# Tying wide products between transposes in TensorE's order: a two-layer decoder trunk

## The chip, the cores and the metric

The kernel runs as one program on one core of a Trainium2 chip; the other cores are idle. The metric is device time in microseconds (us) of one execution, lower is better. Three runs of the kernel before took 705.88, 707.46 and 708.49 us; the median is 707.46.

A core has five instruction queues that matter here: PE (TensorE, the matrix engine), DVE (VectorE), ACT (ScalarE), POOL (GpSimd) and SP (which issues the DMAs). Each queue is served in the order in which the program was written out; an instruction whose operand is not ready holds everything behind it on its engine.

## The reference

512 tokens of width 1024 run through two layers, in F32. Cut to what matters:

```python
def even_layer(x, mem_n, ...):
    h = rms_norm(x, norm_g)
    a_u, a_v, a_g, b_q, b_k, b_v, b_g, m_q, m_g = split_cols(h @ w_in, EVEN_SPLITS)
    y_a = chunked_sgu(gelu(a_u), gelu(a_v), ...) * silu(a_g)       # 4 groups, chunks of 128
    o_b = rms_norm(diff_attention(q, k, v, lam), b_subln) * ...    # 8 heads, two maps each
    y_b = o_b * silu(b_g)
    y_m = memory_attention(m_q, mem_n, ...) * silu(m_g)            # 4 heads over 256 memory tokens
    return x + concatenate([y_a, y_b, y_m]) @ w_out

def odd_layer(x, mem_n, ...):
    h = rms_norm(x, norm_g)
    c_a, c_b, c_g, d_q, d_kv, d_bg, d_g, m_q, m_g = split_cols(h @ w_in, ODD_SPLITS)
    y_c = conformer_conv(c_a, c_b, ...) * silu(c_g)                # causal depthwise conv, 31 taps
    y_d = nsa(d_q, kv, gates, ...) * silu(d_g)                     # compressed, selected and window attention
    y_m = memory_attention(m_q, mem_n, ...) * silu(m_g)
    return x + concatenate([y_c, y_d, y_m]) @ w_out
```

## The kernel before

**Two kinds of products.** F32 accuracy is made from a faster type. A matrix is split into a high part, rounded to F32R, and a low part, the rest (`split`, L375 to L377: the high part on ACT, L376, the low part on DVE, L377; weights in `load_unit`, the high part on ACT, L386, the low part on POOL, L389). One product then is three matmuls into the same bank of PSUM: high x high (L402), high x low (L403), low x high (L404). Their moving operand is 512 columns wide as a rule, in some units 256, 280 or 384. These are the wide products. Beside them stand matmuls whose stationary operand, the one that is loaded into the array before the other streams through, is plain F32 with 128 columns: the transposes (`tr`, L399, 128 moving columns), the products of attention weights and values of layer 0 (L965, 64 columns), the spatial gate (L856) and a few of the convolution's norm. A plain F32 product that is no transpose runs in two passes, so that 3649 matmuls of the program are 3819 in the trace.

**Stages.** Layer 0 opens with projections; then its differential attention (`b_attn`) runs head by head with the remaining projections as filler, memory attention (`m_attn`) with the first part of the output projection, and the rest of that projection. Layer 1 follows the same pattern: projections and convolution, memory attention, then sparse attention (`d_attn`) with gates and output projection as filler. An attention step is a chain over the engines: scores on PE (L927), the masked maximum on DVE (L929, which also empties the bank), exp on ACT (L958 and L1190), a scaling on DVE, transposes on PE (L399), `split`, value products on PE (L965 or L1213). A gate is a projection, a tanh on ACT (L478) and one DVE operation (L479), after which its bank is free.

**What sets the order.** `emit` writes the work as generators that `merge` interleaves by weights (FILL0 and the like). A scheduler then lays out each engine's queue from its own estimate of when an instruction is ready and how long it takes. Data dependences become semaphore waits. SBUF and PSUM are handed out by the kernel's own arenas, so a bank or page that is used again is a dependence too. No line of the kernel before names PE's order as such.

Of the kernel before, what the change touches and what calls it, by code (L numbers as in the profile page):

```python
# [23 lines left out]
F32 = mybir.dt.float32  # L24
F32R = mybir.dt.float32r
# [6 lines left out]
P = 128  # L32
S = 512
DM = 1024
# [248 lines left out]
        self.close()  # L283


def emit(ctx, tc, nc, D, out):
    sbp = ctx.enter_context(tc.tile_pool(name="sb", bufs=1))
    psp = ctx.enter_context(tc.tile_pool(name="ps", bufs=1, space=bass.MemoryType.PSUM))
    words = {k: sum(a * b for c in v.values() for a, b in c) for k, v in PAGES.items()}
# [12 lines left out]
    def banks(d, s, t, o):  # L302
        arenas["p"].deal(512, d=d, s=s, t=t, o=o)

    V, A, G, mm = nc.vector, nc.scalar, nc.gpsimd, nc.tensor.matmul
    dma = nc.sync.dma_start
    act = A.activation

    def f32(t):
        return t.bitcast(F32)  # L310

    def bc(ap, shape):
        return ap.broadcast_to(list(shape))

    def tok(i):
        return slice(i * P, (i + 1) * P)
# [4 lines left out]
    def load_x():  # L321
        for i in range(NT):
            x_t[i] = x_sc([P, DM])
            dma(x_t[i], D["x"][tok(i), :])

    def load_gain(j, sc):
        t = sc([P, DM])
        dma(t, bc(D["norms"][j:j + 1, :], [P, DM]))
        return t
# [3 lines left out]
    for a in range(2):  # L333
        dma(x_t[0][:, a * 512:(a + 1) * 512], D["x"][tok(0), a * 512:(a + 1) * 512])
    gain0 = load_gain(1, start_sc)
    coff = [0]

    def C(shape):
        n = int(np.prod(shape[1:]))
        v = cst_t[:shape[0], coff[0]:coff[0] + n]  # L340
        coff[0] += n
        assert coff[0] <= CONST
        if len(shape) == 3:
            v = v.rearrange("p (a b) -> p a b", a=shape[1])
# [34 lines left out]
    def load_unit(sc, dram, w=DM, eng=None):  # L379
        u = sc([P, 2, DM], F32R, "w")  # L380
        h, l = u[:, 0, :w], u[:, 1, :w]
        with SC() as rs:
            raw = rs([P, w], F32, "raw")
            dma(raw, dram)
            if eng is None:
                act(h, raw, AF.Copy)  # L386
                for a in range(0, w, 512):
                    c = slice(a, min(a + 512, w))
                    G.tensor_tensor(l[:, c], raw[:, c], f32(h[:, c]), SUB)  # L389
            else:  # L390
                split(raw, h, l, eng)
        return h, l

    def load(sc, name):
        i, n = UIDX[name]
        return [load_unit(sc, D["wall"][i + j]) for j in range(n)]

    def tr(o, i, k=P):
        nc.tensor.transpose(o, i, ident[:k, :k])  # L399

    def mm3(o, lh, ll, rh, rl, first, last):
        mm(o, lh, rh, start=first, stop=False)  # L402
# [3 lines left out]
    def h_tile(xt, gain, hs, tk, parts=1):  # L406
        with SC() as sc:
            xs = sc([P, DM])
            ss = sc([P, 2])
            cols = [slice(a * DM // parts, (a + 1) * DM // parts) for a in range(parts)]  # L410
            for a, c in enumerate(cols):
                act(xs[:, c], xt[:, c], AF.Square, accum_out=ss[:, a:a + 1])
            if parts == 2:
                G.tensor_tensor(ss[:, 0:1], ss[:, 0:1], ss[:, 1:2], ADD)
            r = rstd(sc, ss[:, 0:1], 1.0 / DM, 1)
            for c in cols:
                V.scalar_tensor_tensor(xs[:, c], xt[:, c], r, gain[:, c], MUL, MUL)  # L417
            for b in range(2):
                with SC() as pc:
                    p = pc.ps("t", [P, 4, P])  # L420
                    for k in range(4):
                        tr(p[:, k, :], xs[:, (4 * b + k) * P:(4 * b + k + 1) * P])
                    split(p, hs[0][b][:, :, tk], hs[1][b][:, :, tk])
# [90 lines left out]
    def to_keys(sc, t, r, _, h, l):  # L514

        d = sc([P, 4, 2, 64])
        V.tensor_tensor(d, bc(t.unsqueeze(2), [P, 4, 2, 64]),
                        bc(r.unsqueeze(2).unsqueeze(3), [P, 4, 2, 64]), MUL)
        p = sc.ps("t", [P, 4, P])
        for k in range(4):  # L520
            tr(p[:, k, :], d[:, k, :, :].rearrange("p a d -> p (a d)"))
        split(p, h, l)

    def to_queries(sc, q3, r, t, dst):

        nh = t.shape[1]
        V.tensor_tensor(t, q3, bc(r.unsqueeze(2), [P, nh, 64]), MUL)
        p = sc.ps("t", [P, nh // 2, P])
        for k in range(nh // 2):
            tr(p[:, k, :], t[:, 2 * k:2 * k + 2, :].rearrange("p a d -> p (a d)"))  # L530
        for n, q in enumerate(dst):
            q = q.rearrange("p (k a) t -> p a k t", a=2)
            for a in range(2):
                src = p[64 * a:64 * a + 64, 2 * n:2 * n + 2, :]
                act(q[0:64, a], src, AF.Copy)
                V.tensor_tensor(q[64:128, a], src, f32(q[0:64, a]), SUB)
# [815 lines left out]
                     out_part(1, srcs, rev, done)), 1.0)))  # L1352

PAGES = {"f": {"f": [(1024, 10), (512, 18), (16, 40)], "raw": [(1024, 3)]},
         "r": {"x": [(2048, 7)], "w": [(2048, 5)]},
# [20 lines left out]
ARRAYS = ["x", "mem", "wall", "wqb", "vec", "bs", "col", "w1", "w2", "wsT", "norms", "tab"]  # L1378


def build(shapes):
    nc = bacc.Bacc("TRN2", target_bir_lowering=False, num_devices=1)
    D = {n: nc.dram_tensor(f"in_{n}_dram", shapes[n], F32, kind="ExternalInput").ap() for n in ARRAYS}
    out = nc.dram_tensor("out_0_dram", (S, DM), F32, kind="ExternalOutput").ap()
    with tile.TileContext(nc, schedule_with_timeline_sim=True) as tc, ExitStack() as ctx:
        emit(ctx, tc, nc, D, out)
    return nc


# [5 lines left out]
```

## Time and profile before

| | |
|---|---|
| median of three runs | 707.46 us |
| the profiled execution | 707.62 us, its span 705.9 us |
| PE busy | 668.9 us (95%), 3819 matmuls |
| PE weight loads busy | 566.9 us (80%) |
| DVE, POOL, ACT busy | 496.9 (70%), 392.4 (56%), 377.1 us (53%) |
| chain that ended last | PE 70%, DVE 13%, POOL 5%, ACT 5%, issue 3%, DMA 3% |
| mean granted TensorE clock | 0.988 of full speed |

The span runs from the first instruction to the last. A matmul's recorded duration covers its whole way through the array, and matmuls overlap; what one costs PE is read from the distance between starts.

### The profile page before, as it was taken

The numbers are of one execution on the slowest core, as the hardware profiler recorded it, in microseconds if no ns is written. First come the engines' busy times: TensorE is split into PE (matmuls) and PEld (weight loads), VectorE is DVE, ScalarE is ACT, GpSimd is POOL, SyncE is SP. The second block draws the span as 40 slices with busy tenths as digits, with TensorE's granted clock in tenths as the row PEclk, the third lists the DMA queues.
The fourth block names the chain that finished last, engine by engine and source line by source line (L and its number), as shares of the span: only waits on it lengthen the run. The fifth ranks groups of instructions, "written<-read, shape, count | busy, mean of one in ns | idle before, by whom it ended". The sixth has DMA issues, their size and how long they took to land.

```text
span 705.9 us, 11050 instructions
## 1 busy us (share of the span) xinstructions
PE 668.9 (95%) x3819; PEld 566.9 (80%) x3819; DVE 496.9 (70%) x1204; ACT 377.1 (53%) x846; POOL 392.4 (56%) x414
## 2 busy tenths in 40 slices
PE   4999989999999979989989999899999999999997
PEld 3789989878888867878878888777777888788875
DVE  4605668666666875773465978998867776998773
ACT  5345345656455763752453568642346666676541
POOL 3367877474427773245754779965664523421650
PEclk9999999999999997999999999999999999999999
DMA  8532134463323252122322411104021101110121
GB/s 313 175 119 91 60 90 140 131 184 131 103 61 121 84 185 90 61 91 93 122 90 91 149 62 58 61 1 149 33 88 59 61 31 60 54 68 1 61 76 74
DMA packets 22376, 66.56 MB, mean 94 GB/s; under 512 B 3504, under 2 KB 3760, under 8 KB 22320
## 3 DMA queue, kind: packets, MB, share of 16 engines
q1 hardware_dynamic: 22320, 65.86, 28.5%
q8 instruction: 30, 0.49, 0.3%
q14 instruction: 26, 0.21, 0.1%
HBM read 57.46 MB, written 2.10 MB: 84 GB/s over the span
## 4 chain that ended last, share of the span: by engine, by line
PE 70%; DVE 13%; POOL 5%; ACT 5%; issue 3%; DMA 3%; SPq 0%; ACTq 0%; POOLq 0%; DVEq 0%
PE banks L403 18%; PE banks L404 17%; PE banks L402 17%; PE banks L399 6%; DVE arena_r L377 3%; PE banks L927 3%; DMA arena_f<-in_wall_dram 2%; POOL arena_r L389 2%; POOL arena_f L372 2%; PE banks L1213 2%; PE banks L965 2%; ACT arena_r L386 1%; DVE arena_f L929 1%; PE banks L1089 1%; PE banks L1183 1%
## 5 line engine op out<-in xcount | busy, mean ns | idle before, releaser
L389 POOL TENSOR_TENSOR arena_r<-arena_f,arena_r 128x512 fp32r<-128x512 f32 (+1 forms) x174 | 228.8, 1340 | 176.1 <-ACT arena_r L386 172.5
L402 PE MATMUL banks<-arena_r 128*128 128x512 f32 (+2 forms) x784 | 290.5, 375 | 5.4 <-ACT arena_r L386 2.2
L403 PE MATMUL banks<-arena_r 128*128 128x512 f32 (+2 forms) x784 | 290.9, 372 | 1.9 <-POOL arena_r L389 1.3
L404 PE MATMUL banks<-arena_r 128*128 128x512 f32 (+2 forms) x784 | 289.4, 371 | 1.5 <-DVE arena_r L377 1.5
L402 PEld LDWEIGHTS banks<-arena_r 128*128 128x128 f32 x784 | 149.3, 191 | 31.1 <-ACT arena_r L386 3.5
L403 PEld LDWEIGHTS banks<-arena_r 128*128 128x128 f32 x784 | 149.7, 191 | 25.4 <-POOL arena_r L389 2.8
L404 PEld LDWEIGHTS banks<-arena_r 128*128 128x128 f32 x784 | 149.4, 191 | 24.2 <-DVE arena_r L377 2.2
L386 ACT ACTIVATE arena_r<-arena_f 128x1024 fp32r<-128x1024 f32 (+2 forms) x87 | 91.1, 1049 | 75.6 <-PE banks L403 21.3
L399 PE MATMUL banks<-const,arena_f 128*128 128x128 f32 x507 | 84.1, 283 | 16.3 <-DVE arena_f L417 9.4
L377 DVE TENSOR_TENSOR arena_r<-banks,arena_r 128x512 fp32r<-128x512 f32 (+1 forms) x112 | 67.1, 608 | 27.4 <-ACT arena_r L376 26.9
L399 PEld LDWEIGHTS banks<-const,arena_f 128*128 128x128 f32 x507 | 63.0, 146 | 28.9 <-DVE arena_f L417 9.8
L376 ACT ACTIVATE arena_r<-banks 128x512 fp32r<-128x512 f32 (+1 forms) x112 | 57.9, 532 | 52.0 <-PE banks L399 37.0
L929 DVE CUSTOM_DVE_ANT_0 arena_f<-banks,const 128x512 f32<-128x512 f32 (+3 forms) x128 | 60.5, 485 | 33.8 <-PE banks L927 28.2
L372 POOL TENSOR_TENSOR arena_f<-arena_f,const 128x4 f32<-128x4 f32 (+3 forms) x60 | 68.0, 1135 | 3.7
L1262 DVE SCALAR_TENSOR_TENSOR banks<-arena_f,const,banks 128x482 f32<-128x482 f32 (+14 forms) x90 | 66.1, 734 | 1.3
L927 PE MATMUL banks<-arena_r 128*128 128x512 f32 (+7 forms) x192 | 50.8, 338 | 4.5 <-DVE arena_f L929 2.1
L1190 ACT ACTIVATE arena_f<-arena_f 128x256 f32<-128x256 f32 (+3 forms) x64 | 35.7, 559 | 26.0 <-DVE arena_f L929 25.2
L958 ACT ACTIVATE arena_f<-arena_f 128x512 f32<-128x512 f32 (+3 forms) x64 | 35.7, 560 | 24.8 <-DVE arena_f L929 24.4
L657 DVE TENSOR_TENSOR arena_f<-arena_f,banks 128x512 f32<-128x512 f32 x40 | 27.0, 684 | 25.6 <-PE banks L404 25.1
L574 POOL TENSOR_SCALAR arena_f<-arena_f 128x512 f32<-128x512 f32 (+3 forms) x32 | 19.9, 626 | 39.6 <-DVE arena_f L1192 33.7
L927 PEld LDWEIGHTS banks<-arena_r 128*128 128x128 f32 (+1 forms) x192 | 32.8, 190 | 10.6 <-DVE arena_f L929 4.7
L1260 POOL TENSOR_TENSOR arena_f<-arena_f 128x482 f32<-128x482 f32 (+29 forms) x30 | 37.8, 1259 | 2.2 <-ACT arena_f L1259 0.6
(177 smaller groups left out, 811.7 us busy)
## 6 DMA issues: line engine op xcount, KB each, us to landing
arena_f<-in_wall_dram SPq DMA_DIRECT2D x88, 512.0 KB, 3.3
arena_r<-arena_r SPq DMA_DIRECT2D x96, 64.0 KB, 2.0
arena_f<-in_x_dram SPq DMA_DIRECT2D x7, 512.0 KB, 4.5
arena_f<-in_w_dram SPq DMA_DIRECT2D x4, 512.0 KB, 3.7
out_dram<-arena_f SPq DMA_DIRECT2D x8, 256.0 KB, 2.0
arena_f<-in_norms_dram SPq DMA_DIRECT2D x3, 512.0 KB, 3.9
arena_f<-in_mem_dram SPq DMA_DIRECT2D x2, 512.0 KB, 3.3
arena_f<-in_wqb_dram SPq DMA_DIRECT2D x2, 420.0 KB, 3.2
```

Source lines behind the costliest of these rows:

```text
L372: G.tensor_tensor(r, v, mhalf[:parts, :n], ALU.pow)
L376: act(h, src, AF.Copy)
L377: (eng or V).tensor_tensor(l, src, f32(h), SUB)
L386: act(h, raw, AF.Copy)
L389: G.tensor_tensor(l[:, c], raw[:, c], f32(h[:, c]), SUB)
L399: nc.tensor.transpose(o, i, ident[:k, :k])
L402: mm(o, lh, rh, start=first, stop=False)
L403: mm(o, lh, rl, start=False, stop=False)
L404: mm(o, ll, rh, start=False, stop=last)
L927: mm(t[:, a % per, :], q, k[:, :w], start=b == 0, stop=b == len(qk) - 1)
L929: V.tensor_tensor_reduce(e[a], t[:, a % per, :], cmask[:, S - w:], -1.0, -NEG, ADD, ALU.min, nm[:, a:a + 1])
L1262: V.scalar_tensor_tensor(acc[:, z:], hc[:, :S - z], cw[:, f, k:k + 1], acc[:, z:], MUL, ADD)
```

## The change

`mm` and `tr` now pass every matmul through `note`, which writes down its bank, whether its stationary operand is plain F32 with 128 columns, and whether it is a wide product (F32R, 256 moving columns or more). The program is built twice. After the first build `weave` walks through PE's order. Where two plain F32 loads stand next to each other, it looks among the next 24 matmuls for a wide product in another bank that depends on none of those it would pass, and whose last producer off PE stands at least 12 instructions ahead. It ties that product between the two: it must come after the first and before the second. In the second build these ties are given to the scheduler as dependences without a semaphore; all else is scheduled anew.

```diff
+    def note(i, o, l, r):
+        bank = o.offset % words["p"] // 512
+        log[i.ins.name] = (i.ins, bank, l.dtype == F32 and l.shape[-1] == P, r.dtype == F32R and r.shape[-1] >= 256)
+
+    def mm(o, l, r, **k):
+        note(nc.tensor.matmul(o, l, r, **k), o, l, r)
...
     def tr(o, i, k=P):
-        nc.tensor.transpose(o, i, ident[:k, :k])
+        note(nc.tensor.transpose(o, i, ident[:k, :k]), o, i, ident)
...
+REACH, AGE = 24, 12
...
+    left, last, edges = [i.name for i in ins if i.name in log], None, []
+    while left:
+        x = left.pop(0)
+        if log[x][2] and last and log[last][2]:
+            for j, y in enumerate(left[:REACH]):
+                over = [x] + left[:j]
+                if log[y][3] and born.get(y, -1) < pos[x] - AGE and \
+                        all(log[z][1] != log[y][1] and not leads(z, y) for z in over):
+                    edges += [(last, y), (y, x)]
+                    left.pop(j)
+                    break
+        last = x
+    return edges
...
 def build(shapes):
+    edges = []
+    for _ in range(2):
...
+        with tile.TileContext(nc, schedule_with_timeline_sim=True) as tc, ExitStack() as ctx:
+            emit(ctx, tc, nc, D, out, log)
+            for a, b in edges:
+                tc.add_manual_dep(log[b][0], a, IN_ORDER, reason="order of TensorE")
+        edges = weave(nc, log)
     return nc
```

In the rows of the two orders a matmul of the kernel before has the line that asked for it (L399 is a transpose, L402 to L404 the three wide products, L927 scores, L1213 and L965 values). In the changed kernel all matmuls are issued in `note`'s callers: L406 is a transpose, L314 any other matmul, and the output's shape tells them apart. `banks` is PSUM, `arena_r` holds F32R, `arena_f` and `const` plain F32.

PE in layer 0's attention, 131 us into the trace of before; two pairs of transposes with wide products around them:

```order
L965 MATMUL banks<-arena_f 128x64
L399 MATMUL banks<-const,arena_f 128x128 x2
L404 MATMUL banks<-arena_r 128x512
L399 MATMUL banks<-const,arena_f 128x128 x2
L402 MATMUL banks<-arena_r 128x512
L403 MATMUL banks<-arena_r 128x512
L404 MATMUL banks<-arena_r 128x512
```

The same place with the change:

```order
L314 MATMUL banks<-arena_f 128x64
L314 MATMUL banks<-arena_r 128x512
L406 MATMUL banks<-const,arena_f 128x128
L314 MATMUL banks<-arena_r 128x512
L406 MATMUL banks<-const,arena_f 128x128
L314 MATMUL banks<-arena_r 128x512 x2
L406 MATMUL banks<-const,arena_f 128x128
L314 MATMUL banks<-arena_r 128x512
L406 MATMUL banks<-const,arena_f 128x128
```

Each of the four transposes now stands alone between wide products, which came from behind.

PE in the same stage, 213 to 217 us; scores (L927) of two heads, then a projection in 256 columns:

```order
L856 MATMUL banks<-arena_f 128x128 x4
L927 MATMUL banks<-arena_r 128x256
L927 MATMUL banks<-arena_r 128x128
L927 MATMUL banks<-arena_r 128x512 x2
L927 MATMUL banks<-arena_r 128x384
L402 MATMUL banks<-arena_r 128x256
```

With the change:

```order
L314 MATMUL banks<-arena_r 128x128
L314 MATMUL banks<-arena_r 128x512 x2
L314 MATMUL banks<-arena_r 128x256 x12
L314 MATMUL banks<-arena_r 128x384
L314 MATMUL banks<-arena_r 128x256 x29
```

Twelve products of 256 columns moved ahead of the score product of 384; they write a bank that a gate (L479) uses before them. No tie stands here: it is the scheduler's new layout.

PE in layer 1's sparse attention, 557 to 560 us; ahead of these rows stand four score products and four value products:

```order
L399 MATMUL banks<-const,arena_f 128x128 x4
L1213 MATMUL banks<-arena_r 64x256
L1213 MATMUL banks<-arena_r 128x256
L1213 MATMUL banks<-arena_r 64x256
L1213 MATMUL banks<-arena_r 128x256
L399 MATMUL banks<-const,arena_f 128x128 x4
L927 MATMUL banks<-arena_r 128x512 x2
L1213 MATMUL banks<-arena_r 128x256
L927 MATMUL banks<-arena_r 128x512 x2
L402 MATMUL banks<-arena_r 128x512
```

With the change, from the four score products on:

```order
L314 MATMUL banks<-arena_r 128x512 x4
L406 MATMUL banks<-const,arena_f 128x128
L314 MATMUL banks<-arena_r 128x512 x3
L406 MATMUL banks<-const,arena_f 128x128
L314 MATMUL banks<-arena_r 128x512
L406 MATMUL banks<-const,arena_f 128x128 x2
L314 MATMUL banks<-arena_r 64x256
L314 MATMUL banks<-arena_r 128x256
L314 MATMUL banks<-arena_r 64x256
L314 MATMUL banks<-arena_r 128x256
```

The four later score products (three in the row x3 and its neighbourhood, one tied between transposes) now follow the first four almost at once, and the value products come behind them.

## Rows read from the trace of the kernel before

**Rows 1.** The page: the span, and PE's busy time, share and instructions.

```profile
span 705.9 us, 11050 instructions
...
PE 668.9 (95%) x3819; PEld 566.9 (80%) x3819; DVE 496.9 (70%) x1204; ACT 377.1 (53%) x846; POOL 392.4 (56%) x414
```

**Rows 2.** Timeline of PE at 602: start us, us, engine, line, tiles, shape, count.

```profile
601.80 0.60 PE L399 MATMUL banks<-const,arena_f 128*128 128x128 f32 x4
602.15 0.48 PE L403 MATMUL banks<-arena_r 128*128 128x512 f32 x1
602.47 0.39 PE L404 MATMUL banks<-arena_r 128*128 128x512 f32 x1
```

**Rows 3.** Timeline of PE at 130 to 131.

```profile
130.16 0.39 PE L402 MATMUL banks<-arena_r 128*128 128x512 f32 x1
130.39 0.22 PE L927 MATMUL banks<-arena_r 96*128 96x128 f32 x1
130.45 0.44 PE L403 MATMUL banks<-arena_r 128*128 128x512 f32 x1
...
130.90 0.39 PE L399 MATMUL banks<-const,arena_f 128*128 128x128 f32 x2
...
131.36 0.38 PE L399 MATMUL banks<-const,arena_f 128*128 128x128 f32 x2
```

**Rows 4.** Timeline of PE at 221, one transpose between products of 256 columns.

```profile
221.26 0.28 PE L399 MATMUL banks<-const,arena_f 128*128 128x128 f32 x1
...
221.50 0.28 PE L404 MATMUL banks<-arena_r 128*128 128x256 f32 x1
221.61 0.28 PE L402 MATMUL banks<-arena_r 128*128 128x256 f32 x1
```

**Rows 5.** Timeline of PE at 570, scores against compressed keys.

```profile
570.27 1.06 PE L1147 MATMUL banks<-ckt,arena_r 128*128 128x64 f32 x8
571.16 0.29 PE L1148 MATMUL banks<-ccm,identb 128*128 128x256 bf16 x1
```

**Rows 6.** Timeline of PE at 556 to 560.

```profile
556.36 1.09 PE L927 MATMUL banks<-arena_r 128*128 128x512 f32 x4
557.29 0.63 PE L1213 MATMUL banks<-arena_r 128*64 128x256 f32 x4
557.75 0.60 PE L399 MATMUL banks<-const,arena_f 128*128 128x128 f32 x4
...
559.68 0.40 PE L927 MATMUL banks<-arena_r 128*128 128x512 f32 x1
```

**Rows 7.** Timeline of DVE at 558.

```profile
558.16 0.69 DVE L929 CUSTOM_DVE_ANT_0 arena_f<-banks,const 128x512 f32<-128x512 f32 x1
```

**Rows 8.** Timeline of PE at 213 to 215; idle time before, and who ended it.

```profile
213.66 0.74 PE L927 MATMUL banks<-arena_r 96*128 96x512 f32 x2 [0.47 <-DVE arena_f L929]
215.19 0.45 PE L927 MATMUL banks<-arena_r 96*128 96x384 f32 x1 [0.79 <-DVE arena_f L929]
```

**Rows 9.** Timeline of DVE at 215.

```profile
215.65 0.68 DVE L479 SCALAR_TENSOR_TENSOR arena_f<-arena_f,banks 128x512 f32<-128x512 f32 x1
```

**Rows 10.** Timeline of ACT at 214.

```profile
214.14 0.61 ACT L478 ACTIVATE arena_f<-banks 128x512 f32<-128x512 f32 x1
```

**Rows 11.** Timeline of PE at 142.

```profile
142.08 0.33 PE L399 MATMUL banks<-const,arena_f 128*128 128x128 f32 x1 [0.67 <-DVE arena_f L962]
```

**Rows 12.** Timeline of PE at 363.

```profile
363.68 0.66 PE L399 MATMUL banks<-const,arena_f 128*128 128x128 f32 x4 [1.43 <-DVE arena_r L377]
```

**Rows 13.** Timeline of PE at 181.

```profile
181.48 0.42 PE L927 MATMUL banks<-arena_r 96*128 96x384 f32 x1
```

**Rows 14.** Timeline of DVE at 178.

```profile
177.86 0.68 DVE L929 CUSTOM_DVE_ANT_0 arena_f<-banks,const 128x512 f32<-128x512 f32 x1
```

**Rows 15.** Timeline of PE at 94.

```profile
94.41 0.48 PE L927 MATMUL banks<-arena_r 96*128 96x512 f32 x1 [2.12 <-DMA arena_r<-arena_r]
```

**Rows 16.** Windows: busy us of each engine (instructions), granted clock, DMA share, GB/s.

```profile
94.90:98.30 3.40, 3.40 (x18) 3.40 (x17) 1.88 (x5) 1.20 (x3) 2.22 (x3) 0.50 0.37 90
```

More of the change, by code (lines that the diff above doesn't have):

```diff
@@ L283, in __exit__, with emit @@
         self.close()
-def emit(ctx, tc, nc, D, out):
+def emit(ctx, tc, nc, D, out, log):
     sbp = ctx.enter_context(tc.tile_pool(name="sb", bufs=1))
@@ L303, in banks @@
         arenas["p"].deal(512, d=d, s=s, t=t, o=o)
-    V, A, G, mm = nc.vector, nc.scalar, nc.gpsimd, nc.tensor.matmul
+    V, A, G = nc.vector, nc.scalar, nc.gpsimd
     dma = nc.sync.dma_start
     act = A.activation
+    def note(i, o, l, r):
[3 more added lines that the diff above has]
+        note(nc.tensor.matmul(o, l, r, **k), o, l, r)
     def f32(t):
@@ L1352, in emit @@
                      out_part(1, srcs, rev, done)), 1.0)))
+IN_ORDER = mybir.DependencyInfo(mybir.DependencyClass.NoSync, mybir.DependencyReason.DATA)
 PAGES = {"f": {"f": [(1024, 10), (512, 18), (16, 40)], "raw": [(1024, 3)]},
@@ L1378 @@
 ARRAYS = ["x", "mem", "wall", "wqb", "vec", "bs", "col", "w1", "w2", "wsT", "norms", "tab"]
-def build(shapes):
[L1382 to L1386, printed above, removed]
+REACH, AGE = 24, 12
@@ new lines, in weave, with leads @@
+def weave(nc, log):
+    ins = [i for i in nc.all_instructions()]
+    pos = {i.name: n for n, i in enumerate(ins)}
+    after = {i.name: [d for d in i.descendants or () if d in pos] for i in ins}
+    born = {}
+    for i in ins:
+        if i.name not in log:
+            for d in after[i.name]:
+                born[d] = max(born.get(d, -1), pos[i.name])
+    def leads(a, b):
+        seen, todo = {a}, [a]
+        while todo:
+            for d in after[todo.pop()]:
+                if d == b:
+                    return True
+                if d not in seen and pos[d] < pos[b]:
+                    seen.add(d)
+                    todo.append(d)
+        return False
+    left, last, edges = [i.name for i in ins if i.name in log], None, []
[11 more added lines that the diff above has]
+    return edges
@@ new lines, in build @@
+def build(shapes):
+    edges = []
+    for _ in range(2):
+        nc = bacc.Bacc("TRN2", target_bir_lowering=False, num_devices=1)
+        D = {n: nc.dram_tensor(f"in_{n}_dram", shapes[n], F32, kind="ExternalInput").ap() for n in ARRAYS}
+        out = nc.dram_tensor("out_0_dram", (S, DM), F32, kind="ExternalOutput").ap()
+        log = {}
+        with tile.TileContext(nc, schedule_with_timeline_sim=True) as tc, ExitStack() as ctx:
[3 more added lines that the diff above has]
+        edges = weave(nc, log)
```

## The prediction

> **What bounds the kernel now.** I read the page first, then single stretches of TensorE's timeline, then the engine that ended the waits there. The page says PE is busy for 668.9 of 705.9 us [rows 1]; in the chain of waits, the next view, most of the time is PE's own work. Idle PE is 705.9 - 668.9 = 37.0 us in all. So an order of PE's work can pay in two ways only: the same instructions take less time in another neighbourhood, or some of the 37.0 us of waits go. The execution with this span took 707.62 us, 1.7 us around the span; the median of the runs is 707.46, so 0.16 is taken off at the end.
>
> **What the change does.** Counted in the two orders, 611 matmuls load 128 plain F32 columns, and 455 times two of them are direct neighbours; with the change it is 275 times. So 180 neighbours are parted by a product of 256 or more F32R columns. No instruction is added or removed, on any engine. What moves is the order: locally on PE, by a few places on the other engines, and one weight load (I count it from the order) 30 places ahead among SP's DMAs.
>
> **Term 1, the parted loads.** What does a plain load cost in company, and alone? In [rows 2] four transposes start at 601.80 and the product after the next starts at 602.47: 0.67, less one 512-column product of 0.23 (130.16 to 130.39 in [rows 3]), is 0.44, so 0.11 each. In pairs: from 130.90 to 131.36 there are two transposes and one product [rows 3], 0.46 - 0.23 = 0.23, so 0.115 each. Alone between wide products: 221.26 to 221.50, less a 256-column product of 0.12 (221.50 to 221.61), is 0.12 [rows 4]. The cost doesn't fall when a wide product stands beside it: in [rows 2] the product behind the last transpose is entered at 602.15, only 0.02 after the last transpose (601.80 + 3 x 0.11 = 602.13), but the next one comes 0.32 later instead of 0.23. What the transpose seems to save comes back in the product behind it. So these rows exclude a gain, and parting may cost the difference between 0.11 and 0.12: 180 x 0 to 0.01 = 0 to +1.8 us. I take the middle, +0.9.
>
> [...]
>
> **Term 2, waits that the new order makes.** Every product pulled ahead of a transpose must have its operands and its bank by then. For the 203 ties I compared, in the trace of before, the end of the last instruction that the pulled product waits for with the start of the transpose that it now precedes: it is the later of the two in one case alone. The ties themselves are safe. But they push what the scheduler does around them, and two places stand out.
>
> At 559 the order shows score products (L927) ahead of the eight value products (L1213) and the transposes that stood between them and the scores before. The one that began at 559.68 loses from in front of it nine L1213 products of 0.115 (557.29 to 557.75 is four), seven transposes of 0.11 and two products of 0.23: 1.04 + 0.77 + 0.46 = 2.27 us, so it would stand at 557.41 [rows 6]. It needs the bank that DVE L929 reads out until 558.16 + 0.69 = 558.85 [rows 7]: a wait of 1.44. L929 moves ahead on DVE by two places; the soonest it can end is its 0.69 after the end of the four scores, at 556.36 + 1.09 = 557.45, so about 558.15: a wait of 0.75. Queued behind the waiting product are the transposes and L1213 products that filled this hole before; nothing else can fill it. I take the middle, +1.1.
>
> At 215 PE waits 0.79 for DVE L929 [rows 8]. The new order puts twelve 256-column products there, which would begin at 214.23 (the second of the two products at 213.66 begins at 213.66 + 0.74 - 0.40 = 214.00, and takes 0.23); but they need the bank that DVE L479 gives back, at 215.65 + 0.68 = 216.33 [rows 9]: 2.1 us. L479 moves ahead by two places; it still needs ACT L478, which ends at 214.75 [rows 10], so it can't end before 215.43: 1.2 us. Against the 0.79 that goes, this is +0.4 to +1.3; I take +0.8.
>
> **Term 3, waits that go.** At 142.08 a transpose waits 0.67 for DVE L962 [rows 11]. In the new order ten 512-column products come to stand ahead of it and one leaves: 9 x 0.23 = 2.1 us more work in front. They are products of the weight unit whose load moved ahead on SP. The wait is covered: -0.7. (If their load is late, it stays: 0.) At 363.68 PE waits 1.43 for DVE L377 [rows 12]. Ten products come ahead of that transpose, but the first of them waits for the same instruction: I take 0; -1.4 is the other end.
>
> **Sum.** 707.62 + 0.9 + 1.1 + 0.8 - 0.7 = 709.72; less 0.16: 709.6 us. All lower ends together (0, +0.75, +0.4, -0.7 and -1.4) give 706.5, all upper ends (+1.8, +1.44, +1.3, 0, 0) 712.0.
>
> **Rivals.** The first, faster: the load of a parted transpose hides behind the wide product, and the load after it is short. Then it costs what 128 streamed columns cost, 0.06 (130.39 to 130.45, [rows 3]), not 0.11: 180 x 0.05 = 9.0 us less, 698.5. For it speaks the 0.02 from a transpose to the next product; against it that this comes back behind, in every block of [rows 2 to 4], that the lone transpose costs as much, and that F32R loads too follow each other at 0.11 [rows 5]. [...]
>
> The second, slower: products that the scheduler pulls onto a bank not yet free. The place is 181.48, a score product [rows 13]. Counted in the orders, eighteen 512-column products (4.14), three transposes (0.33) and eight double-pass products of 0.22 (1.76) no longer stand ahead of it, four of 0.22 (0.88) come: it moves 5.35 us ahead, to 176.13. Its bank was read out by DVE L929 until 177.86 + 0.68 = 178.54 [rows 14]: a wait of 2.4 if L929 can't follow. A wait of that kind has a second price: after 2.12 us of waiting at 94.41 the granted clock was at the lower level, 1.2 GHz, from 94.9 to 98.3 [rows 15, 16], and 3.4 us at half clock lose 1.7. With the upper ends at 559 and 215 (+0.3 and +0.5) it makes 709.6 + 2.4 + 0.8 + 1.7 = 714.5. It decides if L929, which moves four places ahead on DVE, still ends over 2 us after the product's turn. Against it: those four places are the very work that delayed it.
>
> The third, a little faster: chains that start earlier in the new order end earlier, and the waits at 142, 215 and 363 all go (0.67 + 0.79 + 1.43 = 2.9) with no new ones: 707.46 + 0.9 - 2.9 = 705.5. For it: the release at 363 depends on work that now stands earlier; against it: PE's queue is served in order, and both ends of such a chain move.
>
> That the change does little of what it says is true in part: 275 neighbours remain, because no wide product that was ready and free stood near; for those neither a gain nor a loss is counted.
>
> **How the numbers follow.** A measurement of this kernel tells about 0.5% from no change, 3.54 us: faster is under 703.9, slower over 711.0. The forecast gets 0.47 (within 0.36, slower 0.10, faster 0.01), the first rival 0.08 (faster), the second 0.25 (slower 0.21, within 0.04), the third 0.20 (within 0.14, faster 0.06): faster 0.15, within 0.54, slower 0.31. The range takes in the sum's ends, 706.5 to 712.0, the third rival with waits at other places, and the second: 703.5 to 715.0. It leaves out the first rival and what lies beyond the second.
>
> **What would show it.** Term 1: in the changed profile, a transpose with a wide product on both sides still costs 0.11 to 0.12 (start of the transpose to start of the product after the next, less the product). If it costs about 0.06, the first rival is right and so is a time near 698. Term 2: idle time before the score product near 557 to 559 that DVE L929 ends, and before 256-column products near 214 that DVE L479 ends. Term 3: no wait on L962 near 142. PE's busy time should stay near 669 while the span moves with its idle time. A wait over 2 us between 170 and 220, with a stretch of 1.2 GHz behind it, shows the second rival.

## The result, and the profile after

The changed kernel takes 716.79 us (median of 4 runs, 716.24 to 717.75) against 707.91 of the kernel before beside it: a ratio of 1.0129, 95% interval 1.0104 to 1.0153. It is slower by 8.9 us, and above the range of 703.5 to 715.0. In the changed kernel the lines below `mm` have moved: all products have L314 and all transposes L406, and behind them each line is 7 higher (L936 is L929 before, L969 is L962, L384 is L377, L396 is L389). The profiled execution took 716.86 us.

From the page of the changed kernel, span, engines and chain:

```profile
span 715.1 us, 11045 instructions
PE 676.9 (95%) x3819; PEld 568.5 (79%) x3819; DVE 499.2 (70%) x1204; ACT 376.3 (53%) x846; POOL 390.7 (55%) x414
PE 65%; DVE 14%; POOL 8%; ACT 7%; issue 3%; DMA 3%; SPq 0%; ACTq 0%; POOLq 0%; DVEq 0%
```

Against [rows 1] PE's busy time grew by 8.0 us and its idle time by 1.2 (37.0 to 38.2), with the same 3819 matmuls. A reordering that only makes waits would have left the busy time alone. So the next view is the granted clock by stretch. Both programs are cut at places where PE has done the same work, to within about half a us (the counts differ a little with the order). The columns are the stretch, its length, the busy time and count of each engine, the granted clock, the DMA share and the rate. First the kernel before:

```profile
139.00:181.30 42.30, 40.90 (x226) 34.48 (x226) 27.94 (x74) 25.38 (x61) 26.48 (x28) 1.00 0.54 171
181.30:223.60 42.30, 40.89 (x250) 35.84 (x250) 28.19 (x77) 22.88 (x59) 18.62 (x24) 1.00 0.27 85
223.60:273.70 50.10, 45.27 (x243) 37.77 (x243) 38.06 (x100) 31.26 (x78) 34.44 (x40) 0.90 0.35 116
273.70:316.30 42.60, 40.73 (x275) 34.92 (x274) 30.30 (x58) 24.75 (x62) 15.09 (x15) 1.00 0.26 87
```

and the changed kernel:

```profile
139.00:184.40 45.40, 43.68 (x230) 36.65 (x229) 29.69 (x77) 23.74 (x60) 22.46 (x26) 0.92 0.44 142
184.40:226.00 41.60, 40.66 (x245) 35.57 (x244) 27.78 (x75) 22.68 (x55) 19.12 (x23) 1.00 0.27 84
226.00:281.40 55.40, 48.06 (x245) 38.87 (x244) 39.32 (x100) 31.64 (x80) 32.71 (x40) 0.88 0.32 105
281.40:325.40 44.00, 42.08 (x273) 35.83 (x272) 30.44 (x58) 25.52 (x62) 15.12 (x16) 0.96 0.25 85
```

The four stretches grow by 3.1, -0.7, 5.3 and 1.4 us: together 9.1 of the 9.2 by which the span grew. All of it is lost in layer 0, in the heads of `b_attn` and behind them; from 316 (325) us to the end both take the same. In the first stretch PE is busy 2.8 us longer and the clock is 0.92 instead of 1.00.

The stretches at half clock (granted 0.50 to 0.51) themselves, in the changed kernel (cut at tenths of a us):

```profile
164.80:171.70 6.90, 6.90 (x24) 5.72 (x24) 6.90 (x19) 4.50 (x15) 3.54 (x6) 0.51 0.55 210
257.00:260.40 3.40, 3.29 (x10) 2.71 (x11) 0.62 (x3) 1.79 (x4) 0.00 (x0) 0.50 0.00 0
270.60:280.90 10.30, 8.29 (x24) 5.86 (x25) 6.36 (x21) 4.82 (x17) 4.74 (x10) 0.50 0.21 68
318.40:321.80 3.40, 3.40 (x8) 2.72 (x9) 3.04 (x8) 1.07 (x3) 2.44 (x2) 0.50 0.46 160
502.70:506.20 3.50, 3.00 (x7) 2.19 (x8) 2.83 (x7) 1.12 (x4) 2.81 (x4) 0.51 0.01 2
```

and in the kernel before:

```profile
94.90:98.30 3.40, 3.40 (x18) 3.40 (x17) 1.88 (x5) 1.20 (x3) 2.22 (x3) 0.50 0.37 90
262.10:272.30 10.20, 8.12 (x28) 5.90 (x29) 7.89 (x26) 5.61 (x18) 6.35 (x11) 0.50 0.32 104
494.20:497.60 3.40, 3.07 (x8) 2.20 (x8) 3.36 (x7) 0.00 (x0) 2.77 (x5) 0.50 0.11 34
```

The prediction and the expectations call such a stretch 1.2 GHz. What the trace of the kernel before shows is the granted clock of 0.50 and, in it, products of 512 columns that start 0.43 us apart instead of 0.23, which is 1.2 columns per ns. PE is busy for 24.9 us at half clock, before for 14.6. Half of that is put down here as lost to the clock, which is an estimate (0.20 of the 0.43 are 47%): 12.4 against 7.3 us, +5.1. Over the whole span this leaves 1.2 of idle time and 2.9 in which PE counts as busy at full clock. By place the account is plainer. In the four stretches 10.9 us are lost at half clock against 4.1, +6.8, and PE is idle for 11.9 us against 9.5, +2.4, which is the gain between 226 and 281 us. That makes 9.2, the whole loss. The 2.9 lie ahead of 139 us and behind 325, where both kernels take the same time, and stand against 1.7 less lost at half clock and 1.2 less idle time there. The clock is lower in all four runs of the changed kernel (mean granted clock 0.980 to 0.983) than in 66 of the 68 runs of the kernel before beside the experiments (0.985 to 0.993). What stands ahead of the new stretches is in PE's timeline (start, length, then in brackets the wait and what ended it):

```profile
163.16 0.33 PE L314 MATMUL banks<-arena_r 96*128 96x128 f32 x1 [0.66 <-DVE arena_f L936]
164.25 1.90 PE L314 MATMUL banks<-arena_f 128*128 128x64 f32 x10 [0.76 <-ACT arena_f L945]
216.78 0.74 PE L314 MATMUL banks<-arena_r 96*128 96x512 f32 x2 [0.46 <-DVE arena_f L936]
217.99 1.22 PE L314 MATMUL banks<-arena_r 128*128 128x256 f32 x8 [0.47 <-DVE arena_f L486]
255.85 0.33 PE L406 MATMUL banks<-const,arena_f 128*128 128x128 f32 x1 [1.10 <-DVE arena_r L384]
257.11 0.90 PE L406 MATMUL banks<-const,arena_f 128*128 128x128 f32 x3 [0.93 <-DVE arena_r L384]
316.07 1.39 PE L314 MATMUL banks<-arena_r 128*64 128x128 f32 x13 [1.04 <-DVE arena_r L384]
318.34 2.03 PE L314 MATMUL banks<-arena_r 128*128 128x512 f32 x4 [0.88 <-DVE arena_r L384]
369.21 0.66 PE L406 MATMUL banks<-const,arena_f 128*128 128x128 f32 x4 [0.79 <-DVE arena_r L384]
567.04 1.11 PE L314 MATMUL banks<-arena_r 128*128 128x512 f32 x3 [0.22 <-DVE arena_f L936]
```

Each of the three new stretches (from 164.8, 257.0 and 318.4) begins in or behind a pair of waits of 0.7 to 1.1 us, whose ends lie 1.1 to 2.3 us apart. The one from 270.6 has its counterpart in the kernel before, from 262.1. The rows at 217, 369 and 567 are the places of the prediction's terms 2 and 3: 0.93 at 217 where the kernel before waits 1.26, 0.79 at 369 where it waits 1.43, and a new 0.22 at 567.

### The profile page after: what moved, and what is told of

It reads as the page before. It is cut to its first block, busy times and chain, and to the rows that moved or that the text cites. A ratio compares the mean times of both kernels' runs of the same rounds, so it can differ in the third digit from the quotient of the medians.

```text
span 715.1 us, 11045 instructions
## 1 busy us (share of the span) xinstructions
PE 676.9 (95%) x3819; PEld 568.5 (79%) x3819; DVE 499.2 (70%) x1204; ACT 376.3 (53%) x846; POOL 390.7 (55%) x414
## 4 chain that ended last, share of the span: by engine, by line
PE 65%; DVE 14%; POOL 8%; ACT 7%; issue 3%; DMA 3%; SPq 0%; ACTq 0%; POOLq 0%; DVEq 0%
PE banks L314 60%; PE banks L406 5%; POOL arena_f L379 4%; DVE arena_r L384 3%; DMA arena_f<-in_wall_dram 3%; POOL arena_r L396 2%; ACT arena_r L393 2%; DVE arena_f L936 2%; ACT arena_r L383 1%; DVE arena_f L969 1%; POOL arena_f L377 1%; ACT arena_f L1197 1%; ACT arena_f L965 1%; DVE arena_f L968 1%; DVE banks L1269 1%
## 5 line engine op out<-in xcount | busy, mean ns | idle before, releaser
L314 PE MATMUL banks<-arena_r 128*128 128x512 f32 (+7 forms) x2936 | 618.5, 363 | 15.8 <-DVE arena_r L384 3.1
L314 PEld LDWEIGHTS banks<-arena_r 128*128 128x128 f32 (+2 forms) x2936 | 476.4, 187 | 106.0 <-DVE arena_r L384 6.7
L396 POOL TENSOR_TENSOR arena_r<-arena_f,arena_r 128x512 fp32r<-128x512 f32 (+1 forms) x174 | 224.6, 1316 | 169.1 <-ACT arena_r L393 158.9
L406 PE MATMUL banks<-const,arena_f 128*128 128x128 f32 x507 | 108.5, 285 | 17.3 <-DVE arena_f L424 9.7
L406 PEld LDWEIGHTS banks<-const,arena_f 128*128 128x128 f32 x507 | 67.8, 147 | 29.3 <-DVE arena_f L424 10.1
L384 DVE TENSOR_TENSOR arena_r<-banks,arena_r 128x512 fp32r<-128x512 f32 (+1 forms) x112 | 67.4, 608 | 27.2 <-ACT arena_r L383 26.7
L936 DVE CUSTOM_DVE_ANT_0 arena_f<-banks,const 128x384 f32<-128x384 f32 (+3 forms) x128 | 60.7, 484 | 31.0 <-PE banks L314 27.8
L965 ACT ACTIVATE arena_f<-arena_f 128x512 f32<-128x512 f32 (+3 forms) x64 | 35.6, 558 | 26.3 <-DVE arena_f L936 25.7
L377 POOL TENSOR_SCALAR arena_f<-arena_f 128x4 f32<-128x4 f32 (+3 forms) x60 | 16.7, 279 | 41.9 <-DVE arena_f L511 15.5
L314 PEld LDWEIGHTS banks<-arena_f 128*128 128x128 f32 (+1 forms) x256 | 36.1, 182 | 4.0 <-ACT arena_f L945 1.3
L314 PE MATMUL banks<-arena_f 128*128 128x64 f32 (+2 forms) x256 | 36.6, 270 | 1.0 <-ACT arena_f L945 1.0
L384 DVE TENSOR_TENSOR arena_r<-arena_f,arena_r 128x256 fp32r<-128x256 f32 (+1 forms) x44 | 29.7, 700 | 3.5 <-ACT arena_r L383 3.4
L383 ACT ACTIVATE arena_r<-arena_f 128x256 fp32r<-128x256 f32 (+1 forms) x44 | 19.2, 468 | 16.8 <-PE banks L314 7.9
L969 DVE SCALAR_TENSOR_TENSOR arena_f<-arena_f 128x512 f32<-128x512 f32 (+3 forms) x32 | 25.1, 786 | 0.6
```

Source lines behind the costliest of these rows:

```text
L314: note(nc.tensor.matmul(o, l, r, **k), o, l, r)
L383: act(h, src, AF.Copy)
L384: (eng or V).tensor_tensor(l, src, f32(h), SUB)
L406: note(nc.tensor.transpose(o, i, ident[:k, :k]), o, i, ident)
L936: V.tensor_tensor_reduce(e[a], t[:, a % per, :], cmask[:, S - w:], -1.0, -NEG, ADD, ALU.min, nm[:, a:a + 1])
L965: act(e[m], e[m], AF.Exp, bias=nm[:, m:m + 1], scale=-1.0, accum_out=l[:, i, m:m + 1])
```

## The experiments

Fourteen kernels ran, in four groups. Each median is compared with runs of the kernel before on the same chip. Most hold PE's order: the program is built once to learn it, and built again with each matmul bound behind the one ahead of it. The other engines are laid out anew around it, so that their order can still move.

**Ties without a new order, a new order without ties, and half the ties.** `tie_only` moves the 203 products in PE's order of before and nothing else of PE; `untie` puts them back in the changed order (as far as dependences let them); `early` and `late` keep the first 116 or the last 87 ties and leave the rest to the scheduler.

```diff
 # tie_only, in place of edges = weave(nc, log); cut
+ties = weave(nc, log)
+pe = [i.name for i in nc.all_instructions() if i.name in log]
+for (last, y), (_, x) in zip(ties[::2], ties[1::2]):
+    pe.remove(y)
+    pe.insert(pe.index(x), y)
+edges = list(zip(pe, pe[1:]))
 # early, late
-edges = weave(nc, log)
+edges = weave(nc, log)[:232]      # late: [232:]
```

> TensorE keeps the order of the kernel before, written out as a chain, and only the 203 tied products are moved, each to its place in front of the load that it parts; nothing else of TensorE is moved. Theory A (the ties cost nothing by themselves; the loss is the scheduler's new order around them, whose waits of about 1 us open stretches at 1.2 GHz): 706 to 711 us, TensorE busy 667 to 671, no 1.2 GHz stretch that the kernel before has not. Rival B (a parted load costs more than one in a row): 714 to 719, busy 675 to 679, spread evenly over the 203 places at about 44 ns each. Rival C (a tied product is taken before its bank or operand is there, wherever the rest stands): 711 to 715, with waits at the tied products themselves.

> The converse: TensorE has the order of the changed kernel, but every tied product is put back behind the loads that it was pulled past, as far as dependences allow (neighbours 422, against 455 before and 275 changed). Theory A (the layout loses, not the ties): 714 to 719, with the 1.2 GHz stretches near 165, 257 and 318 us mostly kept. Rival B (the parted loads lose): 706 to 710, busy 668 to 671. Rival C (products taken too early): 707 to 711, since the products are back.

> As the changed kernel, but with the first 116 of the 203 ties only (those up to about 330 us); after that the scheduler goes on as it will. Theory A: the three new 1.2 GHz stretches lie before 330 us, so nearly all of the loss stays: 713.5 to 717. Rival B (each tie costs the same 44 ns): 116 of 203 ties, 712 to 714.

> As the changed kernel, but with the last 87 ties only (from about 330 us on), so that the first 330 us are the kernel before's. Theory A: 706.5 to 710, with the 1.2 GHz stretches up to 330 us where the kernel before has them. Rival B (each tie costs the same 44 ns): 87 of 203 ties, 711 to 713.

Measured: `tie_only` 724.39 (ratio 1.0229, 1.0206 to 1.0252), `untie` 721.56 (1.0189, 1.0162 to 1.0217), `early` 715.56 (1.0103, 1.0082 to 1.0123), `late` 707.91 (1.0005, 0.9990 to 1.0021).

`late` and `early` settle the place: 87 ties from 330 us on cost nothing that can be measured, the first 116 cost nearly all of it, and `early` has the changed kernel's pairs of waits and, 0.1 us earlier, its four stretches from 164.8 to 318.4 again. That speaks against a price for each tie. `tie_only` and `untie` went against theory A, and against B and C as well: both are slower than the kernel whose order they start from. Their idle PE is 47.5 and 46.7 us, against 37.0 before and 38.2 after. PE's busy time in `tie_only`, 675.1 us, is what B forecast, but 4.9 of the 6.2 that it grew by are lost at half clock. No wait over 0.2 us behind the start stands there at a wide product between two plain loads, but for the one at 94 that the kernel before has too [rows 15]. The waits come later, for instance 2.13 us at 570 where the kernel before has none: five wide products that stand between the scores and that value product before are gone from there. Not every wait is of this kind. At 143 `tie_only` waits 1.83 where the kernel before has 0.67 [rows 11], with as many products ahead of it; there VectorE ends L969 about 1 us later, since two of its maxima (L936) now run first. At 368 of its 1204 places VectorE runs another kind of operation than in the kernel before. So `tie_only` and `untie` changed more than PE's order, and what the ties cost alone is not shown. Nor is it shown why the changed kernel's idle time grows so much less.

**Which ties, and waits filled with repeated work.** `mid` keeps only the 38 ties between 150 and 230 us, `third` the 28 between 230 and 330. `fill_after` and `fill_before` let PE repeat matmuls in its waits; the order of all its others is held.

```diff
 # fill_after, cut
+FILL = [(786, 6, 896, 'again'), (896, 7, 787, 'again'), (1307, 6, 1230, 'again'), (1230, 8, 1152, 'again')]
+    # matmul number i is issued c times more, placed ahead of number `before`
+    def idle(n, kind, again):
+        for i, c, before, k in FILL:
+            if junk is not None and (i, k) == (n, kind):
+                junk[before] = [again() for _ in range(c)]
```

> As the changed kernel, but only the 38 ties that lie between about 150 and 230 us. Theory A (the loss is made where the new order brings waits and 1.2 GHz stretches, and one of these places is 163 to 171 us): waits of 0.6 to 0.8 us near 163 us, a 1.2 GHz stretch behind them, 709.5 to 713. Rival B (each tie costs about 44 ns): 38 ties are 1.7 us, 708.5 to 710. Rival D (the place near 163 us depends on ties from before 150 us, which are left out here): no wait there, 706.5 to 709.

> As the changed kernel, but only the 28 ties that lie between about 230 and 330 us. Theory A: the pair of waits near 256 us with its 1.2 GHz stretch, and the second one near 318 us, come back: 709.5 to 713. Rival B (44 ns for each tie): 28 ties are 1.2 us, 708 to 709.5. Rival D (these waits need what the earlier ties moved): 706.5 to 709.

> The changed kernel, TensorE held in its order; in four of its waits (0.66 us at 163.2, 0.76 at 164.3, 1.10 at 255.9, 0.93 at 257.1) TensorE repeats work that it has just done (6 transposes, 7 products of 128 columns, 6 of 384, 8 transposes: 27 instructions that change nothing and whose results are read only after the wait). Theory A (half of the loss is the granted clock, which falls because of these waits): the stretches at 1.2 GHz from 164.8 and 257.0 are gone, and with them 3.4 and 1.7 us: 710.5 to 713.5. Rival E (the waits themselves cost, the clock falls for another reason, or the repeats push the work behind them): 716 to 719, stretches still there.

> The kernel before, TensorE held in its order, with repeats in the three waits that stand ahead of its 1.2 GHz stretches: 19 transposes of the identity in the wait of 2.12 us at 94.4, 20 repeated products of 256 columns in that of 2.69 at 262.5, 12 repeated transposes in that of 1.39 at 493.5. Theory A: the three stretches go, which held 7.3 us of lost work: 700 to 703. Rival E: 707 to 710, stretches still there or moved.

Measured: `mid` 713.98 (1.0097, 1.0068 to 1.0126), `third` 709.89 (1.0041, 1.0021 to 1.0061), `fill_after` 715.75 (1.0121, 1.0080 to 1.0162), `fill_before` 708.61 (1.0015, 0.9989 to 1.0041).

`mid` alone brings the waits near 165 us and the half-clock stretch behind them. `third` brings a wait of 2.10 at 251 and a stretch from 250.4, and at 310 and 312 the same pair of waits that the changed kernel has at 316 and 318, but here at full clock:

```profile
310.12 1.40 PE L314 MATMUL banks<-arena_r 128*64 128x128 f32 x13 [1.04 <-DVE arena_r L384]
312.40 3.91 PE L314 MATMUL banks<-arena_r 128*128 128x512 f32 x16 [0.88 <-DVE arena_r L384]
308.00:320.00 12.00, 10.07 (x65) 8.05 (x64) 8.20 (x15) 6.93 (x19) 7.58 (x6) 1.00 0.39 132
```

By their medians `mid` and `third` together cost 9.6 us and `early` with all early ties 8.1, which the intervals do not tell apart. `fill_after` took the waits and the stretch at 256 away, but at 165.6 a wait of 0.57 was left, and a stretch came from 167.2, with a wait of 0.86 inside it at 169.0. The stretch at 318 went too, although its two waits, which were not filled, stand there as before (1.04 and 0.88). `fill_before` lost the stretches at 94.9 and 494.2 and got new ones at 215.3 and 314.3, behind waits that the kernel before has too, at full clock. So where waits are filled the stretch can go, another can come behind waits that stood there all along, and the time stays. Theory A was right that stretches stand behind waits and wrong on the gain. In `fill_before` the 20 repeats did not even fill their wait: one VectorE operation took 4.08 us (before 1.59, of which 0.6 is its own) and ended 0.4 behind a run of seven GpSimd subtractions:

```profile
256.13 8.74 POOL L403 TENSOR_TENSOR arena_r<-arena_f,arena_r 128x512 fp32r<-128x512 f32 x7
261.21 4.08 DVE L976 SCALAR_TENSOR_TENSOR arena_f<-arena_f 128x384 f32<-128x384 f32 x1
265.80 0.44 PE L413 MATMUL banks<-const,arena_f 128*128 128x128 f32 x2 [2.82 <-DVE arena_r L550]
```

**The price of a parted load by itself, and VectorE behind GpSimd.** The rows above gave theory F: VectorE stands still while GpSimd subtracts, and PE waits for VectorE. In the kernel before, two VectorE operations of a scaling start 1.9 us and more behind the start of GpSimd's pair of subtractions, and only the first is held (0.69 for 0.21):

```profile
155.74 2.54 POOL L389 TENSOR_TENSOR arena_r<-arena_f,arena_r 128x512 fp32r<-128x512 f32 x2
157.60 0.69 DVE L961 SCALAR_TENSOR_TENSOR arena_f<-arena_f,const 128x1 f32<-128x1 f32 x1
158.33 0.35 DVE L962 SCALAR_TENSOR_TENSOR arena_f<-arena_f 128x128 f32<-128x128 f32 x1
```

In the changed kernel the same two start 0.5 and 1.4 us behind that start, and both are held:

```profile
157.31 2.53 POOL L396 TENSOR_TENSOR arena_r<-arena_f,arena_r 128x512 fp32r<-128x512 f32 x2 [0.30 <-ACT arena_r L393]
157.85 0.77 DVE L968 SCALAR_TENSOR_TENSOR arena_f<-arena_f,const 128x1 f32<-128x1 f32 x1
158.66 1.33 DVE L969 SCALAR_TENSOR_TENSOR arena_f<-arena_f 128x128 f32<-128x128 f32 x1
```

`apart_after` and `apart_before` let the subtraction wait for such an operation, with PE's order held:

```diff
+HOLD = mybir.DependencyInfo(mybir.DependencyClass.Sync, mybir.DependencyReason.DATA)
+for p, d in APART:                 # (a GpSimd subtraction, a VectorE operation)
+    tc.add_manual_dep(subs[p], d, HOLD, reason="GpSimd starts behind VectorE")
```

> A kernel of its own that leaves out the whole layer and writes products of one input block; TensorE's order is held. After 96 wide products of 512 columns for a start: 16 times 8 transposes of 128 columns (plain F32 operand loaded) and 8 wide products in blocks; then 128 times one transpose and one wide product by turns; then 128 transposes in a row. Theory A (parting a load hides nothing): 8 and 8 take 8 x 0.107 + 8 x 0.229 = 2.69 us, a block of 16 the same by turns, 43 us for either stretch of 256. Rival 1 of the prediction (the load of a transpose hides behind the wide product ahead of it): by turns 8 x (0.229 + 0.028) = 2.06 us for 16, 33 us for 256. Rival B (a parted load costs 44 ns more): 3.04 us for 16, 48.6 for 256.

> The changed kernel with TensorE's order held and one thing added: at five places GpSimd's subtraction (L396) waits for the VectorE operation with two operands in SBUF that it would hold up (L969 at 158.7, 164.5 and 267.3 us, L384 at 251.7 and 316.8). Theory F (the waits of TensorE at 163 to 164, 256 to 257, 269 and 316 to 318 us go back to VectorE standing still, about 1 us each time, until a running subtraction of GpSimd ends; the waits then bring the 1.2 GHz stretches): VectorE's four-fold durations there go back to 0.34, 0.74, 0.6 and 0.41 us, the waits shrink by 3 to 4 us together, and part of the 6.8 us lost at 1.2 GHz goes with them: 706 to 712. Rival G (the order of the products is to blame, VectorE would be waited for anyway): waits stay within 1 us of what they were, 715 to 718.

> The same in the kernel before, TensorE's order held, six places: GpSimd's subtraction (L389) waits for L962 at 140.7 and 260.4 us, L377 at 248.7 and 309.1, L417 at 360.7, L576 at 614.3. Theory F: TensorE's waits of 0.67 us at 142, 0.49 at 251, 2.69 at 262.5, 1.47 at 310.7, 1.43 at 363.7 and 0.87 at 617 lose 4 to 6 us together, and the 10 us at 1.2 GHz from 262 (5 us of lost work) goes or shortens: 697 to 703. Rival G: 706 to 709. Rival H (GpSimd, now later, holds up the products that need its result): 709 to 714, with new waits on L389.

`small`, by windows (blocks of 8 and 8; by turns; transposes alone; columns as above):

```profile
28.25:71.72 43.47, 43.47 (x257) 37.27 (x256) 0.00 (x0) 0.00 (x0) 0.00 (x0) 1.00 0.00 1
71.72:115.53 43.81, 43.81 (x258) 34.99 (x257) 0.00 (x0) 0.00 (x0) 0.00 (x0) 1.00 0.00 1
115.53:129.40 13.87, 13.87 (x129) 13.87 (x127) 0.00 (x0) 0.00 (x0) 0.00 (x0) 1.00 0.01 1
```

128 parted transposes cost 0.34 us more than 128 in blocks, 0.003 each. The first rival would have shown 33 us in the second row by the expectation (37 by the prediction's own 0.06 for a parted load), rival B 48.6. There parting a load neither saved nor cost more than that.

`apart_after` took 712.35 (1.0074, 1.0049 to 1.0099), some 4 us less than the changed kernel; `apart_before` 709.02 (1.0025, 1.0009 to 1.0042). In `apart_after` (lines behind L396 one higher still) the orders of PE, VectorE and ScalarE are those of the changed kernel. At two of the five places the durations fell as theory F says (0.35 for 1.33, 0.75 for 1.72), at the others VectorE was held as long as before (1.59 for 1.59, 2.37 for 2.35, and 4.96 for 4.97 over the eight L384 at 247):

```profile
159.68 0.35 DVE L970 SCALAR_TENSOR_TENSOR arena_f<-arena_f 128x128 f32<-128x128 f32 x1
160.11 1.28 POOL L396 TENSOR_TENSOR arena_r<-arena_f,arena_r 128x512 fp32r<-128x512 f32 x1 [0.48 <-DVE arena_f L970]
164.18 0.33 PE L314 MATMUL banks<-arena_r 96*128 96x128 f32 x1 [0.66 <-DVE arena_f L937]
164.56 0.75 DVE L970 SCALAR_TENSOR_TENSOR arena_f<-arena_f 128x512 f32<-128x512 f32 x1
247.33 4.96 DVE L384 TENSOR_TENSOR arena_r<-arena_f,arena_r 128x256 fp32r<-128x256 f32 x8
251.06 1.88 PE L314 MATMUL banks<-arena_r 128*128 128x512 f32 x7 [0.46 <-POOL arena_r L396]
254.54 0.55 PE L407 MATMUL banks<-const,arena_f 128*128 128x128 f32 x3 [0.93 <-DVE arena_r L384]
262.55 1.59 DVE L970 SCALAR_TENSOR_TENSOR arena_f<-arena_f 128x384 f32<-128x384 f32 x1
311.88 2.37 DVE L384 TENSOR_TENSOR arena_r<-arena_f,arena_r 128x256 fp32r<-128x256 f32 x2
```

Its time lies at the upper end of the range that F gave, 0.35 us above it, and not by F's sum: the idle time is 38.3 us, as without the edit (0.66 at 164.2 stays, 0.76 behind it falls to 0.36, 1.10 at 256 to 0.34, and 0.46 on GpSimd comes at 251). What went are the stretches at 164.8, 257.0 and 318.4; one at 95.4 came; the lost work is 6.8 us instead of 12.4. At 318.4 the edit can't be the reason: the pair of waits stands there as before (1.05 and 0.89). In `apart_before` five of the six places came free (the one at 309 did not), and the wait of 2.69 fell to 1.73, that of 1.43 to 0.41. Others grew: 0.93 at 142 and 1.53 at 250, both on GpSimd, which was rival H, and 1.72 at 267 on VectorE.

**Half the hold, and a fresh order without any tie.** Still open was whether the waits come from VectorE's holds or from the new order. GpSimd's subtraction in pieces of 256 columns instead of 512 would, by the author's estimate, hold VectorE for half as long; a piece of 256 then took 0.775 us on average, one of 512 takes 1.327 in the changed kernel. `fine_after` and `fine_before` hold PE's order, `fine_free` is the kernel before with this one edit, all engines scheduled anew. The edit:

```diff
-for a in range(0, w, 512):
-    c = slice(a, min(a + 512, w))
+for a in range(0, w, 256):
+    c = slice(a, min(a + 256, w))
     G.tensor_tensor(l[:, c], raw[:, c], f32(h[:, c]), SUB)
```

> The changed kernel, TensorE's order held; GpSimd's subtraction (L396) is cut into pieces of 256 columns instead of 512, so that a VectorE operation that meets one can be held for some 0.65 us at most instead of 1.3. Theory F (VectorE held by GpSimd makes the waits): the time that VectorE is held falls from 39 us to about half over the kernel, TensorE's waits between 160 and 320 us from about 14 us to 10 or 11, and with them some of the work at 1.2 GHz: 709 to 714. Rival G (the order of the products is to blame): 715.5 to 718. Rival I (171 more starts of GpSimd make it late for the products that need it): over 718.

> The same in the kernel before, TensorE's order held: pieces of 256 columns on GpSimd (L389). Theory F: VectorE is held half as long (18 us instead of 37), TensorE's waits at 262.5, 310.7 and 363.7 (5.6 us together) lose 1.5 to 2.5 us, and the 10 us at 1.2 GHz behind the first may go: 702 to 706. Rival G: 706.5 to 708.5. Rival I: 709 or more.

> The kernel before with the pieces of 256 columns and nothing held: the scheduler orders all engines anew. If the pieces help by themselves (theory F) and the new order is no worse: 702 to 707. If any new order of the scheduler is as likely to fall into waits as the changed kernel's was: anywhere from 705 to 718.

Measured: `fine_after` 715.81 (1.0126, 1.0096 to 1.0156), `fine_before` 709.62 (1.0033, 1.0010 to 1.0057), `fine_free` 715.44 (1.0121, 1.0098 to 1.0145).

GpSimd is busy for 420 us instead of 391 to 392, and the holds (an estimate: what VectorE's operations beside a subtraction take beyond the shortest of the same line and shape) fell by a quarter and not by half, from about 38 to 29 us after and from 37 to 28 before. `fine_after` takes as long as the changed kernel, but not for the same reasons. In its profiled execution the three new stretches are gone here too, and 8.0 us are lost at half clock instead of 12.4. Idle time grew by 3.8 us, most of it at one place:

```profile
365.07 1.11 PE L406 MATMUL banks<-const,arena_f 128*128 128x128 f32 x4 [3.48 <-DVE arena_r L384]
```

The changed kernel waits 0.79 there. With GpSimd busy for longer and VectorE's order moved as well, this run doesn't settle how much of the loss is theory F's. The pair that tells is `fine_before` and `fine_free`: the same instructions, no tie, and 5.8 us between them, from the order of the queues alone. This fresh order costs, against the kernel before, what the change did (1.0121 and 1.0129). Not every one does: `late` and `third` are laid out anew behind their first tie and take 707.91 and 709.89.

## Why the prediction was wrong

The prediction was right in its mechanism for the loads and wrong in time: the sum counted the new order at four places and held the rest for unchanged.

**Term 1 was right.** Parting 180 neighbours was put at +0.9 (0 to +1.8); at 0.003 each it is +0.5. The first rival (698.5) is out, by `small` and by `late`.

**Term 2 failed at both places.** At 559 a wait of 0.75 to 1.44 was forecast; the only wait left near that place is 0.22, at 567. At 215 the forecast wait for the bank that VectorE L479 gives back is there (217.99, on L486) but 0.47 long and not 1.2 to 2.1; with 0.46 at 216.78 the place has 0.93 where [rows 8] had 1.26. Both were worked out by moving an engine's rows by its work and leaving the releaser nearly where it was; the releaser moved along.

**Term 3 was right at 142** (the wait is gone) and nearly so at 363: 0.79 instead of 1.43 [rows 12], inside its 0 to -1.4. By the named places alone the kernel would have become faster: 0.5 + 0.2 - 0.3 - 0.7 - 0.6 is -0.9.

**The step that failed** is "The ties themselves are safe. But they push what the scheduler does around them, and two places stand out." The first half held: in the changed kernel's trace none of the waits ahead of the new stretches stands at a wide product between two plain loads. What they push is not two places. The 9.1 us are at 139 to 184 and 226 to 325 us, where no term stood: 2.4 us are idle time, mainly new waits of 0.7 to 1.1 us, and 6.8 are lost at half clock (0.50 to 0.51), in stretches that begin in or behind them. The prediction took two places for the whole of what the ties push; the price of a re-layout had no term of its own, and `fine_free` shows its size without any tie, 5.8 us over `fine_before`.

**The clock was mis-sized.** "PE's busy time should stay near 669" failed by 8.0 us, 5.1 of them half-clock work. The second rival had this course, a wait and a half-clock stretch behind it as at 94 [rows 15, 16], between 170 and 220. Its place was wrong: between 170 and 182 us the longest wait after is 0.30, at 179.46. So was the size of the wait, over 2 us: the three new stretches stand at pairs of 0.7 to 1.1. It priced one stretch at 1.7; these three cost 6.8.

**The range** was built of named places and one stretch, so its upper end, 715.0, was the second rival's 714.5. `mid`, `early`, `fine_free` and the change itself lie at 714.0 to 716.8.

**What stays open:** which property of an order makes it one of 707 or one of 716, and why a wait has a half-clock stretch behind it in one trace and not in another. VectorE's holds take part in where the waits fall: `apart_after` won back some 4 of the 9 us with two of its five places freed. How much of the rest is theirs was not shown, since no kernel freed all five or held VectorE's order while the pieces were halved. No kernel that ran beats the one before.

## What to carry to other kernels

Where a scheduler lays out the queues, an edit that adds order edges is two changes: price the edge, and price a fresh layout separately, by a placebo that reorders without the edge's purpose. Hold the order of the engine in question when one thing is to be measured, but expect that a product moved by hand can be missing where it stood, and that the other engines' orders move. See in the trace whether an edit took hold at each place that it names. And look at the granted clock of each stretch before explaining busy time that grew with the same instructions.

## What the runs showed of the hardware

**The clock fell in or behind waits, but not behind the same wait in every trace.** All 53 stretches at half clock (0.50 to 0.51) in the fifteen traces of the whole kernel begin in a wait of PE or at most 2.1 us behind its end. The wait of 2.1 to 2.4 us at 94 to 95 stands in fourteen of these traces; the clock fell at it in eight, the kernel before among them [rows 15, 16], and not in six, among them the changed one. The pair of 1.0 to 1.1 and 0.9 us at 316 and 318 has a stretch in the changed kernel and in `early`, and none in `untie`, `third`, `fill_after` and `apart_after`. One kernel's own time spread with its clock: `fine_before` took 704.55 us at a mean clock of 0.993 and 712.38 at 0.981, and the runs of the kernel before beside the first three groups average 705.5 at 0.993 (7 runs), 706.7 at 0.990 (18) and 707.9 at 0.988 (17).

**Some VectorE operations with all operands in SBUF took longer beside a GpSimd subtraction, and none with an operand in PSUM.** In the changed kernel 44 of the 147 of the first kind that overlap a subtraction are over 0.1 us longer than the shortest of the same line and shape, before 41 of 156; of the second kind, none of 237 and none of 248. A scaling of 128x128 (L969) took 0.34 to 0.35 us with GpSimd idle (3 of them), and 1.33 and 1.35 beside a subtraction (2); the one of 1.33 ended 0.15 behind GpSimd's pair. The 128x512 L377 from a bank took 0.67 to 0.69 beside a subtraction (23) and with GpSimd idle (33). In all it is about 37 us in the kernel before and 38 after, by the estimate above, so it was there all along. The 4.08 us in `fill_before`, where that shape takes 0.62 in the changed kernel with GpSimd idle, lie beside a run of seven subtractions of 1.25 on average: more than one of them fell into it.
